# A delta-rule mixer: two of three blocks of its output gates move from ahead of the features into the solutions, states and outputs

## The chip, the core and the metric

The kernel runs on one core of a Trainium2 chip. The metric is the device time in microseconds (us) of one execution of the whole program, median of the runs. The profiles are of single executions; times in them count from the start of the profiled span.

## The reference

The program computes two two-layer transformer blocks for 256 tokens and 1024 channels in float32. The change lies in the mixer of the last layer, a gated delta rule with 8 heads of 128 channels; behind it come a mixture of experts and the final norm. Cut to what matters:

```
def gdn_mixer(h, w_in, conv_w, a_log, dt_bias, out_norm, w_out):
    proj = h @ w_in
    qkv, z, b, a = jnp.split(proj, ...)
    qkv = jax.nn.silu(causal_conv(qkv, conv_w))
    q, k, v = jnp.split(qkv, ...)
    q, k = l2_norm(q) * GDN_DK ** -0.5, l2_norm(k)
    beta = jax.nn.sigmoid(b)
    g = -jnp.exp(a_log) * jax.nn.softplus(a + dt_bias)
    o = chunk_gated_delta(q, k, v, g, beta)
    o = rms_norm(o, out_norm) * jax.nn.silu(z)
    return o @ w_out
```

Within chunk_gated_delta the cumulated decay g enters every part. The output gates silu(z) are needed only for the last product, ahead of w_out.

## The kernel before, in words

Every large product is written as three matmuls on rounded parts: an operand x is split into hi (ScalarE cast, L591) and lo = x - hi (VectorE, L592), and mm3 (L682 to L684) adds hi·hi, hi·lo and lo·hi. Weights are streamed in one fixed order (weight_order): raw tiles of up to 1024 columns are loaded by the sync queue into 8 buffers, and split in that order into 4 pairs of buffers whi and wlo, at most 4 tiles ahead of the matmuls. A split waits until the matmuls on the pair four places earlier are over.

The mixer is the function gdn. Its stages, in the order of the code:

- The normed input of the second 128 tokens is still being split (hi, lo) while the projection gdn_z begins. Its columns come in three blocks: one of 344, which are 328 gate columns and the 16 columns of b and a, and two of 348 gate columns. Each block has 8 steps (k), a step has two mm3, one for each half of the tokens (b). The results go through Silu into sz.
- From the 16 columns the decay chain is computed: the copy ab, beta by Sigmoid, then ga, ge by Abs and Exp, gl by a polynomial log1p on VectorE (L733 to L736), and g. Two matmul lines on TensorE (L2296, L2297) sum g over the tokens.
- Features (feats): six groups for k, v and q, with convolution, norm and transposes, by gdn_in weights; in between, piecewise (drip), the inverses of the triangular matrices.
- early: with the inverses done, solve for both chunks, state, correct, each for heads 0 to 3 and 4 to 7, as `four` (L2096: four 128x128 matmuls in float32, which the trace shows as 8). Then outputs(0), scales(0).
- outputs(4), scaled(0) (L2255, o times gates), scales(4), turns(0) (L2375), and then the product with gdn_out, which begins with lead.

scales ends on GpSimd with a product of the gates sz and the norm's factor (L2251), for columns 0 to 511 of sz in scales(0).

Each engine runs its own instructions in the order in which they stand. A scheduler sets that order when the program is built, from the code's order and its own estimates; it may interleave work of neighbouring parts. It put the first matmuls of the second gate block between the last ones of the first.

Of the kernel before, what the change touches and what calls it, by code (L numbers as in the profile page):

```python
# [14 lines left out]
AF = mybir.ActivationFunctionType  # L15
# [171 lines left out]
def weight_order(where, part):  # L187

    n = lambda pack: range(len(where[pack]))
    down = lambda pack: [(pack, i, where[pack][i][1] // D) for i in n(pack)]  # L190
    up = lambda pack, k=4: [(pack, i, k) for i in n(pack)]
    if part == "m0":
        first = [("ab_in", i, 8, k0) for k0 in (0, 4) for i in AB_ORDER[:FIRST]]
        return first + [("ab_in", i, 4 if i in (8, 9, 15, 16) else 8) for i in AB_ORDER[FIRST:]] + up("ab_out")
    if part == "f0":
        o = []
        for fh in range(2):
            o += [("ffn0_in", 11 * fh + j, 8) for j in range(11)]
            o += [("ffn0_out", 6 * fh + i, FF0_SPLITS[i % 3][1]) for i in range(6)]
        return o  # L200
    if part == "m1":
        return up("attn_in") + down("attn_out")
    if part == "m2":
        return up("mla_in") + up("mla_kvb", 2) + up("mla_qb") + down("mla_out")
    if part == "m3":
        return up("gdn_z") + [("gdn_in", i, 8) for i in (*range(4, 12), *range(4))] + down("gdn_out")
    if part == "f3":
        return [o for e in range(8) for o in up(f"moe_in{e}")[:10] + [(f"moe_in{e}", 10, 8)] + down(f"moe_out{e}")]
    return up(f"ffn{part[1]}_in")[:2] + up(f"ffn{part[1]}_in", 8)[2:] + down(f"ffn{part[1]}_out")
# [302 lines left out]
class Kern:  # L512
# [451 lines left out]
    def down(self, a, KC, pack, gate, job, early, pool, first=None, begun=None):  # L964

        self.tail = pool, pack, (KC - TAIL) * D
        if KC == 8:
            lead, ws, acc = begun  # L970
        else:
            acc = [[self.ps() for _ in range(2)]]
            kn = [w // D for _, w in self.where[pack]]
            ws = (w for i, n in enumerate(kn) for w in self.wk(pack, i, n))
        acc.append([self.ps() for _ in range(2)])
        mm = lambda k, w, b, hs=(0, 1): self.down_mm(a, KC, k, w, acc, b, hs)
        if KC == 8:
            for k in range(2):
                mm(k, lead[k], 1)
            if first:  # L980
                first()
        else:
            for k in range(KC - TAIL):
                w = next(ws)
                for b in range(2):
                    mm(k, w, b)
                if k == 0 and first:
                    first()
                if k in AF2:
                    self.fill()  # L990
            self.fill_all()
        last = list(enumerate(self.take(ws), KC - TAIL))
        if KC > 8:
            self.ahead(WBUFS)
        for k, w in last:
            mm(k, w, 0)
        for h in range(2):
            self.resid(self.x[:, 0], gate, h, acc[0][h])
            job.run(0, job.SQ0 + h)
        if not job.late:  # L1000
            job.run(0, job.SCALED)
        if KC == 8:
            for k in range(2, KC - TAIL):
                mm(k, lead[k], 1)
            self.ahead(WBUFS)
        for h in range(2):
            for k, w in last:
                early.get((h, k), int)()
                mm(k, w, 1, (h,))
            self.resid(self.x[:, 1], gate, h, acc[1][h])  # L1010
            job.run(1, job.SQ0 + h)
        job.run(1, job.R)
# [1057 lines left out]
    def gdn(self, mods, job):  # L2070
        nc = self.nc
        vec, act, pe, gp = nc.vector, nc.scalar, nc.tensor, nc.gpsimd
        H = 8
        with ExitStack() as es:
# [133 lines left out]
            def drip():  # L2208

                if running:  # L2210
                    r_ = running.pop(0)
                    if not next(r_, 1):
                        running.append(r_)
# [42 lines left out]

            def early():

                while running:
                    drip()  # L2260
                for f in (lambda h0: solve(0, h0), state, lambda h0: solve(1, h0), correct):
                    for h0 in (0, 4):
                        f(h0)
                outputs(0)
                scales(0)

            with ExitStack() as es2:
# [2 lines left out]
                h = job.hi, job.lo  # L2270
                h2 = job.tiles
                ab = self.t(hp, [P, 2, 2, H], "ab")
                zo = 0
                for n, z0 in enumerate((696, 0, 348)):
                    zn = (328, 348, 348)[n]
                    w = self.where["gdn_z"][2 * n][1] // 4
                    for b, acc in enumerate(self.proj(h, "gdn_z", 2 * n, w, range(2), job if n == 0 else None)):
                        act.activation(sz[:, b, z0:z0 + zn], acc[:, :zn], AF.Silu)
                        if n == 0:
                            act.copy(ab[:, b], acc[:, zn:zn + 16].rearrange("p (a h) -> p a h", a=2))  # L2280

                act.activation(beta, ab[:, :, 0], AF.Sigmoid)
                a, e, l = (self.t(hp, [P, 2, H], n) for n in ("ga", "ge", "gl"))
# [398 lines left out]
```

## Time and profile before

| what | value |
|---|---|
| median of 3 runs | 2060.82 us (2057.07 to 2062.36) |
| profiled execution, its time | 2066.18 us |
| profiled execution, its span | 2064.5 us |
| TensorE busy | 1989.5 us (96%) |
| VectorE busy | 1498.6 us (73%) |
| ScalarE busy | 1125.5 us (55%) |
| GpSimd busy | 215.3 us (10%) |
| chain that ended last | PE 79%, DVE 8%, DMA 4%, ACT 3% |

The profiled execution took 5.4 us more than the median of the runs. PE is TensorE, PEld its loading of stationary operands, DVE VectorE, ACT ScalarE, POOL GpSimd. A matmul's duration includes the way through the array, so matmuls in a row overlap: what one costs is the distance from its start to the next start. The delta-rule mixer lies between about 1405 and 1620 us.

### The profile page before, as it was taken

What the parts mean: (1) busy time and instruction counts of PE and PEld (TensorE: products, weight loads), DVE (VectorE), ACT (ScalarE), POOL (GpSimd) and SP (SyncE); (2) the same over time, 40 slices, a digit from 0 to 9 for tenths busy, and PEclk for the clock granted to TensorE, in tenths of its full rate; (3) what the DMA queues carried; (4) which work ended last, traced back from release to release, by engine and by line L of the source; (5) the groups of instructions that cost most, each with busy time, mean ns of one, the idle gap of its engine ahead of it and who ended that gap; (6) DMA issues with size and microseconds to landing.
All of it is one profiled execution on the core that took longest, in us unless ns stands there. A gap on an engine that the chain in (4) does not pass through costs nothing.

```text
span 2064.5 us, 31402 instructions
## 1 busy us (share of the span) xinstructions
PE 1989.5 (96%) x11674; PEld 1672.6 (81%) x11674; DVE 1498.6 (73%) x2378; ACT 1125.5 (55%) x1863; POOL 215.3 (10%) x359
## 2 busy tenths in 40 slices
PE   7999999999999999899998999999999899999997
PEld 4877877888888887689987779988898788878775
DVE  2667555796463358778886678877777799988996
ACT  3564462633223246764446764447645587878775
POOL 0000043000000002300001000000402201010101
PEclk8999987999999999999999999999999899999998
DMA  7313255376564233059994249995332579999995
GB/s 293 123 41 115 100 183 206 106 249 212 184 201 134 87 96 123 1 186 325 330 329 167 89 156 332 327 328 199 103 104 67 177 264 337 332 323 331 333 353 196
DMA packets 116642, 420.24 MB, mean 204 GB/s; under 512 B 13016, under 2 KB 13400, under 8 KB 116480
## 3 DMA queue, kind: packets, MB, share of 16 engines
q1 hardware_dynamic: 114640, 412.23, 57.6%
q0 software_dynamic: 976, 3.29, 0.5%
q10 hardware_dynamic: 864, 2.62, 0.3%
q8 instruction: 94, 1.54, 0.3%
q14 instruction: 68, 0.56, 0.1%
HBM read 417.04 MB, written 1.05 MB: 203 GB/s over the span
## 4 chain that ended last, share of the span: by engine, by line
PE 79%; DVE 8%; DMA 4%; ACT 3%; issue 3%; POOL 2%; SPq 0%; POOLq 0%; DVEq 0%; ACTq 0%
PE ps L682 22%; PE ps L683 21%; PE ps L684 21%; DMA raw<-in_w_ada_dram 3%; DVE wlo L592 2%; PE ps L801 2%; PE ps L1590 1%; PE ps L2096 1%; PE ps L2138 1%; DMA raw<-in_w_ffn_out_dram 1%; POOL tiny L692 1%; PE ps L2454 1%; PE ps L2568 1%; PE ps L1611 1%; PE ps L1848 1%
## 5 line engine op out<-in xcount | busy, mean ns | idle before, releaser
L592 DVE TENSOR_TENSOR wlo<-raw,whi 128x1024 fp32r<-128x1024 f32 (+1 forms) x589 | 708.3, 1223 | 171.4 <-ACT whi L591 162.7
L591 ACT CAST whi<-raw 128x1024 fp32r<-128x1024 f32 (+1 forms) x589 | 602.9, 1040 | 364.9 <-PE ps L684 178.1
L682 PE MATMUL ps<-hi,whi 128*128 128x256 f32 x832 | 239.1, 287 | 0.0
L683 PE MATMUL ps<-lo,whi 128*128 128x256 f32 x832 | 235.7, 283 | 0.0
L684 PE MATMUL ps<-hi,wlo 128*128 128x256 f32 x832 | 235.7, 283 | 0.0
L682 PE MATMUL ps<-h_hi,whi 128*128 128x512 f32 (+1 forms) x584 | 221.7, 381 | 1.9 <-ACT h_hi L591 1.9
L845 DVE SCALAR_TENSOR_TENSOR raw<-raw,acc 128x1024 f32<-128x1024 f32 x128 | 156.3, 1222 | 91.7 <-DMA raw<-in_w_ada_dram 91.2
L683 PE MATMUL ps<-h_lo,whi 128*128 128x512 f32 (+1 forms) x584 | 221.1, 379 | 0.0
L684 PE MATMUL ps<-h_hi,wlo 128*128 128x512 f32 (+1 forms) x584 | 221.0, 378 | 0.0
L682 PEld LDWEIGHTS ps<-hi,whi 128*128 128x128 f32 x832 | 159.8, 192 | 1.2
L684 PEld LDWEIGHTS ps<-hi,wlo 128*128 128x128 f32 x832 | 159.8, 192 | 0.2
L683 PEld LDWEIGHTS ps<-lo,whi 128*128 128x128 f32 x832 | 159.8, 192 | 0.1
L683 PE MATMUL ps<-wlo,hh 128*128 128x512 f32 (+1 forms) x384 | 147.0, 383 | 2.6 <-DVE wlo L592 2.5
L682 PE MATMUL ps<-whi,hh 128*128 128x512 f32 (+1 forms) x384 | 145.4, 379 | 0.0
L684 PE MATMUL ps<-whi,hl 128*128 128x512 f32 (+1 forms) x384 | 144.4, 376 | 0.0
L682 PEld LDWEIGHTS ps<-h_hi,whi 128*128 128x128 f32 x584 | 110.2, 189 | 23.4 <-ACT h_hi L591 2.0
L683 PEld LDWEIGHTS ps<-h_lo,whi 128*128 128x128 f32 x584 | 110.3, 189 | 21.9 <-DVE h_lo L592 1.7
L684 PEld LDWEIGHTS ps<-h_hi,wlo 128*128 128x128 f32 x584 | 110.2, 189 | 20.2
L683 PEld LDWEIGHTS ps<-wlo,hh 128*128 128x128 f32 x384 | 72.3, 188 | 21.0 <-DVE wlo L592 8.6
L682 PEld LDWEIGHTS ps<-whi,hh 128*128 128x128 f32 x384 | 72.4, 189 | 13.6 <-ACT hh L591 0.3
L682 PE MATMUL ps<-whi,hi 128*128 128x512 f32 (+3 forms) x208 | 80.5, 389 | 3.0 <-ACT hi L591 2.6
L684 PEld LDWEIGHTS ps<-whi,hl 128*128 128x128 f32 x384 | 72.4, 188 | 12.8
(608 smaller groups left out, 4011.1 us busy)
## 6 DMA issues: line engine op xcount, KB each, us to landing
raw<-in_w_ada_dram SPq DMA_DIRECT2D x192, 512.0 KB, 5.1
raw<-in_w_moe_in_dram SPq DMA_DIRECT2D x170, 512.0 KB, 5.7
raw<-in_w_ffn_in_dram SPq DMA_DIRECT2D x132, 512.0 KB, 5.5
raw<-in_w_moe_out_dram SPq DMA_DIRECT2D x88, 512.0 KB, 5.8
raw<-in_w_ffn_out_dram SPq DMA_DIRECT2D x64, 512.0 KB, 5.7
raw<-in_w_ab_in_dram SPq DMA_DIRECT2D x33, 512.0 KB, 4.6
raw<-in_w_gdn_in_dram SPq DMA_DIRECT2D x24, 512.0 KB, 4.5
raw<-in_w_attn_in_dram SPq DMA_DIRECT2D x12, 512.0 KB, 3.8
```

The lines of the kernel that those rows point to most:

```text
L591: self.first = self.nc.scalar.copy(hi, src)
L592: return self.nc.vector.tensor_tensor(out=lo, in0=src, in1=hi.bitcast(F32), op=ALU.subtract)
L682: mm(out, a[0], b[0], start=start, stop=False)
L683: mm(out, a[0], b[1], start=False, stop=False)
L684: return mm(out, a[1], b[0], start=False, stop=stop)
L692: self.rooted = vec.tensor_tensor(out=y, in0=v, in1=self.mhalf[:, :n], op=ALU.pow)
L801: self.moded = nc.tensor.matmul(pa[32 * g:32 * g + 32, :], self.cs[:, k, :], rw[k // 2][:, k % 2, :], start=k < 4, stop=k >= 4)
L845: nc.vector.scalar_tensor_tensor(out=t, in0=w, scalar=1.0, in1=c, op0=ALU.mult, op1=ALU.mult, accum_out=out[:, k, v:v + 1])
L1590: pe.matmul(pO[:, n], Ws[dr][:, b], mv[:, b, hd], start=True, stop=True)
L1611: pe.matmul(pS[:, b], k[:, s], q[:, s], start=True, stop=True)
L1848: pe.matmul(po[0][64 * u:64 * u + 64, n], v[:, kb, c:c + 64], PTs[u][:, kb].rearrange("p g t -> p (g t)"), start=kb == 0, stop=kb == 3)
L2096: pe.matmul(p[:, i], *f(h0 + i), start=True, stop=True)
```

## The change

The weight order and the code move blocks two and three of gdn_z behind the weights of gdn_in. The first block stays where it was. The other two become a generator, rest, whose pieces are one step (six matmuls, two mm3) each; the last piece of a block also issues its two Silu. early draws one piece after each drip and after each of the eight calls of solve, state and correct, and draws all that is left behind outputs(0) and ahead of scales(0).

```diff
@@ -203,7 +203,8 @@
     if part == "m2":
         return up("mla_in") + up("mla_kvb", 2) + up("mla_qb") + down("mla_out")
     if part == "m3":
-        return up("gdn_z") + [("gdn_in", i, 8) for i in (*range(4, 12), *range(4))] + down("gdn_out")
+        z = up("gdn_z")
+        return z[:2] + [("gdn_in", i, 8) for i in (*range(4, 12), *range(4))] + z[2:] + down("gdn_out")
     if part == "f3":
         return [o for e in range(8) for o in up(f"moe_in{e}")[:10] + [(f"moe_in{e}", 10, 8)] + down(f"moe_out{e}")]
     return up(f"ffn{part[1]}_in")[:2] + up(f"ffn{part[1]}_in", 8)[2:] + down(f"ffn{part[1]}_out")
@@ -2256,12 +2257,17 @@
 
             def early():
 
+                gates = rest()
                 while running:
                     drip()
+                    next(gates, None)
                 for f in (lambda h0: solve(0, h0), state, lambda h0: solve(1, h0), correct):
                     for h0 in (0, 4):
                         f(h0)
+                        next(gates, None)
                 outputs(0)
+                for _ in gates:
+                    pass
                 scales(0)
 
             with ExitStack() as es2:
@@ -2270,14 +2276,23 @@
                 h = job.hi, job.lo
                 h2 = job.tiles
                 ab = self.t(hp, [P, 2, 2, H], "ab")
-                zo = 0
-                for n, z0 in enumerate((696, 0, 348)):
-                    zn = (328, 348, 348)[n]
-                    w = self.where["gdn_z"][2 * n][1] // 4
-                    for b, acc in enumerate(self.proj(h, "gdn_z", 2 * n, w, range(2), job if n == 0 else None)):
-                        act.activation(sz[:, b, z0:z0 + zn], acc[:, :zn], AF.Silu)
-                        if n == 0:
-                            act.copy(ab[:, b], acc[:, zn:zn + 16].rearrange("p (a h) -> p a h", a=2))
+                for b, acc in enumerate(self.proj(h, "gdn_z", 0, 344, range(2), job)):
+                    act.activation(sz[:, b, 696:], acc[:, :328], AF.Silu)
+                    act.copy(ab[:, b], acc[:, 328:].rearrange("p (a h) -> p a h", a=2))
+
+                def rest():
+
+                    for n in (1, 2):
+                        accs = [self.ps()[:, :348] for _ in range(2)]
+                        for k, w in enumerate(w for i in range(2) for w in self.wk("gdn_z", 2 * n + i, 4)):
+                            for b in range(2):
+                                self.mm3(accs[b], [z[b][:, k] for z in h], w, k == 0, k == 7)
+                            if k < 7:
+                                yield
+                        for b in range(2):
+                            act.activation(sz[:, b, 348 * n - 348:348 * n], accs[b], AF.Silu)
+                        yield
+
 
                 act.activation(beta, ab[:, :, 0], AF.Sigmoid)
                 a, e, l = (self.t(hp, [P, 2, H], n) for n in ("ga", "ge", "gl"))
```

The names of lines below are those of the kernel before on the side of before and those of the changed kernel on its side: L682 to L684 become L683 to L685, L2096 becomes L2097, L2296 becomes L2311, L591 and L592 become L592 and L593.

TensorE at the end of the first gate block. Before, the last step of the third block (348 columns), then the sums over g, then the first features (256 columns):

```order
L683 MATMUL ps_13184<-wlo_13188,hi_6579 128x348
L684 MATMUL ps_13184<-whi_13187,lo_6580 128x348
L2296 MATMUL ps_13283<-g_12972,grp_c_2397_12969 128x8
L2297 MATMUL ps_13283<-g_12972,grp_c_2397_12969 128x8
L2296 MATMUL ps_13283<-g_12972,grp_c_2397_12969 128x8
L2297 MATMUL ps_13283<-g_12972,grp_c_2397_12969 128x8
L682 MATMUL ps_13293<-hi_6579,whi_13205 128x256
L683 MATMUL ps_13293<-lo_6580,whi_13205 128x256
```

Of the change, the same place:

```order
L683 MATMUL ps_12992<-whi_12866,hi_6579 128x344
L684 MATMUL ps_12992<-wlo_12867,hi_6579 128x344
L685 MATMUL ps_12992<-whi_12866,lo_6580 128x344
L2311 MATMUL ps_13113<-g_12972,grp_c_2397_12969 128x8
L2312 MATMUL ps_13113<-g_12972,grp_c_2397_12969 128x8
L2311 MATMUL ps_13113<-g_12972,grp_c_2397_12969 128x8
L2312 MATMUL ps_13113<-g_12972,grp_c_2397_12969 128x8
L683 MATMUL ps_13123<-hi_6579,whi_13127 128x256
```

The 96 matmuls of 348 columns that stood ahead of the sums over g are gone from this place: the sums follow directly on the first block (344 columns), and the features still stand behind them.

ScalarE at the same place, from the copy ab of the second 128 tokens to the Exp of the decay chain. Before (casts of 696 columns are of gdn_z):

```order
L2280 COPY ab_12990<-ps_12992 128x16
L591 CAST whi_13111<-raw_13109 128x696
L591 CAST whi_13129<-raw_13127 128x696
L2282 ACT_TABLE_LOAD
L2282 ACTIVATE beta_12976<-ab_12990 128x16
L591 CAST whi_13147<-raw_13145 128x696
L2286 ACTIVATE ge_13261<-ga_13260 128x16
L2287 ACT_TABLE_LOAD
L2287 ACTIVATE ge_13261<-ge_13261 128x16
```

Of the change (casts of 1024 columns are of gdn_in):

```order
L2281 COPY ab_12990<-ps_12992 128x16
L592 CAST whi_13145<-raw_13143 128x1024
L2297 ACT_TABLE_LOAD
L2297 ACTIVATE beta_12976<-ab_12990 128x16
L2301 ACTIVATE ge_13091<-ga_13090 128x16
L2302 ACT_TABLE_LOAD
L2302 ACTIVATE ge_13091<-ge_13091 128x16
```

Of three casts between the copy and the Exp one is left, a wider one; both table loads stay.

VectorE and ScalarE behind outputs(0). Of the change, ScalarE from the last feature-sized copy of outputs(0) (kT holds o) past the Silu of the third block to the copies kqT that outputs(4) reads:

```order
L2244 COPY kT_12983<-ps_15057 128x512
L724 ACTIVATE w_2747_15146<-kT_12983 128x512
L724 ACTIVATE w_2748_15149<-kT_12983 128x512
L592 CAST whi_15091<-raw_15089 128x1024
L592 CAST whi_15109<-raw_15107 128x1024
L592 CAST whi_15127<-raw_15125 128x1024
L2293 ACTIVATE sz_12971<-ps_15069 128x348
L2293 ACTIVATE sz_12971<-ps_15070 128x348
L592 CAST whi_15276<-raw_15274 128x1024
L2379 COPY kqT_12984<-ps_15157 128x4x128
L2379 COPY kqT_12984<-ps_15163 128x4x128
```

Before, the first kqT copy stood between the two Square activations (w), with no cast and no Silu in this place. VectorE, of the change, from the second half of outputs(0) to the masks LS of outputs(4):

```order
L2246 TENSOR_TENSOR kT_12983<-kT_12983,ps_15063 128x512
L725 TENSOR_REDUCE tiny_2746_15145<-w_2747_15146 128x4
L725 TENSOR_REDUCE tiny_2746_15145<-w_2748_15149 128x4
L593 TENSOR_TENSOR wlo_15092<-raw_15089,whi_15091 128x1024
L593 TENSOR_TENSOR wlo_15110<-raw_15107,whi_15109 128x1024
L593 TENSOR_TENSOR wlo_15128<-raw_15125,whi_15127 128x1024
L2256 TENSOR_TENSOR sz_12971<-kT_12983,sz_12971 128x512 x2
L593 TENSOR_TENSOR wlo_15277<-raw_15274,whi_15276 128x1024
L2132 TENSOR_TENSOR LS_12985<-ps_15170,LS_12985 128x4x128
L2132 TENSOR_TENSOR LS_12985<-ps_15176,LS_12985 128x4x128
```

Before, no subtraction of weights (wlo) stood here, and the first LS stood ahead of the first product sz. On TensorE the eight steps of the second block stand one by one behind the eight groups of solve, state and correct; the eight steps of the third block, 48 matmuls, stand in one piece between outputs(0) and the transposes and matmuls of outputs(4).

## Rows read from the trace of the kernel before

**Rows 1.** Three stretches: length, PE, PEld, DVE, ACT, POOL busy, PEclk, DMA share, GB/s

```profile
1416.00:1433.20 17.20, 17.20 (x111) 16.94 (x110) 12.57 (x28) 14.41 (x24) 0.00 (x0) 1.00 0.80 268
1433.20:1557.60 124.40, 120.43 (x1506) 115.34 (x1506) 89.86 (x187) 67.20 (x125) 28.91 (x36) 0.99 0.35 108
1557.60:1579.00 21.40, 20.51 (x178) 19.79 (x176) 15.14 (x27) 11.68 (x22) 4.78 (x8) 1.00 0.16 50
```

**Rows 2.** Timeline of TensorE, end of the output gates

```profile
1419.44 0.32 PE L682 MATMUL ps<-whi,hi 128*128 128x348 f32 x1
...
1432.25 0.32 PE L684 MATMUL ps<-whi,lo 128*128 128x348 f32 x1
1432.41 0.28 PE L2296 MATMUL ps<-g,grp_c 128*128 128x8 f32 x2
```

**Rows 3.** Groups of instructions by shape, 1405 to 1436

```profile
...
L682 PE MATMUL ps<-whi,hi 128*128 128x348 f32 x32 | 10.2, 322 | 0.0
...
L592 DVE TENSOR_TENSOR wlo<-raw,whi 128x696 fp32r<-128x696 f32 x8 | 7.0, 882 | 2.1 <-ACT whi L591 1.9
L591 ACT CAST whi<-raw 128x696 fp32r<-128x696 f32 x8 | 6.1, 771 | 0.0
...
L592 DVE TENSOR_TENSOR wlo<-raw,whi 128x1024 fp32r<-128x1024 f32 x4 | 4.8, 1222 | 0.9 <-ACT whi L591 0.9
L591 ACT CAST whi<-raw 128x1024 fp32r<-128x1024 f32 x4 | 4.2, 1048 | 1.0 <-PE ps L684 1.0
```

**Rows 4.** Timeline of VectorE, the decay chain up to g

```profile
1417.11 0.42 DVE L592 TENSOR_TENSOR lo<-w,hi 128x256 fp32r<-128x256 f32 x1
...
1424.25 0.17 DVE L733 TENSOR_SCALAR gl<-ge 128x16 f32<-128x16 f32 x1 [0.76 <-ACT ge L2287]
...
1427.85 0.17 DVE L2292 SCALAR_TENSOR_TENSOR g<-ga,tiny 128x16 f32<-128x16 f32 x1
```

**Rows 5.** Timeline of ScalarE, the same chain

```profile
1418.87 0.17 ACT L2280 COPY ab<-ps 128x16 f32<-128x16 f32 x1
...
1420.40 1.28 ACT L2282 ACT_TABLE_LOAD   x1
...
1424.00 0.22 ACT L2287 ACTIVATE ge<-ge 128x16 f32<-128x16 f32 x1
```

**Rows 6.** Timeline of TensorE, solutions to the first weights of gdn_out

```profile
1559.78 1.95 PE L2096 MATMUL ps<-vb,LS 128*128 128x128 f32 x16
1561.57 1.33 PE L2096 MATMUL ps<-vb,kt 128*128 128x128 f32 x10
...
1578.09 1.06 PE L2096 MATMUL ps<-vb,LS 128*128 128x128 f32 x8
1581.73 1.27 PE L2096 MATMUL ps<-vb,LS 128*128 128x128 f32 x8 [2.58 <-DVE LS L2131]
1582.65 0.46 PE L872 MATMUL ps<-idr,ghi 128*128 128x128 f32 x1
...
1586.09 1.85 PE L313 MATMUL ps<-grp_vecs,mod 128*128 128x8 f32 x16
```

**Rows 7.** Timelines of VectorE, ScalarE and GpSimd, the same stretch

```profile
1579.56 1.51 DVE L2255 TENSOR_TENSOR sz<-kT,sz 128x512 f32<-128x512 f32 x1 [2.48 <-POOL sz L2251]
1580.99 0.68 DVE L2131 TENSOR_TENSOR LS<-ps,LS 128x512 f32<-128x512 f32 x1
...
1574.56 0.59 ACT L2364 COPY kqT<-ps 128x512 f32<-128x512 f32 x1
...
1578.49 2.04 POOL L2251 TENSOR_TENSOR sz<-sz,tiny 128x512 f32<-128x512 f32 x2
```

**Rows 8.** Timeline of TensorE; then windows: length, PE busy, PEclk, DMA share, GB/s

```profile
1465.73 0.63 PE L2363 MATMUL ps<-grp_cc,kt 128*128 128x128 f32 x4 [2.19 <-DVE kt L2345]
...
1467.00:1468.00 1.00, 1.00 (x6) 0.50 0.01 4
...
1583.00:1584.00 1.00, 1.00 (x7) 0.50 0.00 0
```

## Prediction

> **What bounds the kernel now.** I read the windows of the mixer first, then the timelines of TensorE, ScalarE and VectorE at the two places that the change touches, then the clock of the stretches behind waits. The reader is to see that TensorE sets the pace on both sides of the move. While the gates' last two blocks are projected it is busy for all of 17.2 us, through the features and inverses nearly always, and through the solutions, states and outputs for 20.51 of 21.40 us [rows 1]. So the place that the work goes to has almost no room: 0.89 us there, and behind it one wait, from the end of the eight matmuls at 1578.09 (1578.99, at 0.112 each) to 1581.73, 2.74 us [rows 6]. The place that it leaves is where the decay chain runs: the sums over g stand at 1432.41, right behind the last gate matmul [rows 2], and g had been ready since 1428.02 [rows 4]. The sums never waited, because some 16 us of gate matmuls lay over the chain. That cover is what the change takes away, and the features are queued behind the sums.
>
> **The head, step by step.** The chain starts when the first block's second half is done, and this waits for VectorE's last piece of lo, ended at 1417.53 [rows 4]. Ahead of that piece stand two weight subtractions, and ahead of them a cast; they become 1024 wide in place of 696: 1.048 - 0.771 = 0.28 us for the cast, and 2 x (1.222 - 0.882) = 0.68 us for the subtractions [rows 3]. So lo, the end of the block and the copy ab come about 0.9 us later: ab ends at 1419.04 + 0.9 = 1419.9 [rows 5].
>
> From there to the Exp took 1424.00 - 1419.04 = 4.96 us, with ScalarE always at work [rows 5]. Three casts of 0.771 us go (2.31) and one of 1.048 stays [rows 3]: 3.70 us, the two table loads (1.28 each) among them. Exp starts at 1423.6. From the first step of log1p to the end of g took 1428.02 - 1424.25 = 3.77 us [rows 4], a subtraction of 0.882 us inside, which leaves: 2.9 us. With 0.25 us between Exp and log1p [rows 4, 5], g is there at 1426.75 and the sums can start at about 1427.0. TensorE ends the first block at about 1419.4 (0.9 us later than the block ended) and stands for some 7.6 us. It takes up the sums 1432.41 - 1427.0 = 5.4 us earlier than before, though 15.4 us of matmuls have gone. Bounds: 6.3 us earlier if lo comes no later, 4.5 us if the wider cast and subtractions of the next tiles also stand in the way.
>
> Behind such a wait the clock counts. After a wait of 2.19 us ended at 1465.73 the granted clock was 0.50, the 1.2 GHz level, in 1467 to 1468, and again in 1583 to 1584 behind the wait of 2.74 us [rows 6, 8]. Its price: the 16 groups from 1582.65 to 1586.09 took 3.44 us [rows 6]; at the 2.4 GHz level it would have been half, so one such stretch costs 1.7 us. I charge the features one: +1.7, from 0 to 2.6 (half of a stretch one and a half times as long). Features and inverses keep TensorE busy, VectorE and ScalarE have the same work, so I carry the shift unchanged to the solutions: **-5.4 + 1.7 = -3.7 us.**
>
> **The tail.** The added work: 80 matmuls from 1419.44 to 1432.25 [rows 2] are 0.160 us each; 3 x 32 of them [rows 3] are 15.4 us. Eight steps stand one by one between the groups of solve, state and correct, and these follow each other without a wait already (16 matmuls in 1561.57 - 1559.78 = 1.79 us, [rows 6]), so each step of 0.96 us pushes the next group out. The eight weight splits move too, 6.1 us on ScalarE and 7.0 us on VectorE [rows 3]; they lie between the same engines' copies, TensorE is later than they are, and ScalarE (11.68 of 21.40) and VectorE (15.14) have room [rows 1], so I price them at nothing; if they came in the way they would cost up to one split per block, 2 x 0.9 us. Their loads stand behind those of gdn_in in the queue, with 8 buffers, and the DMA share is 0.16 in that stretch [rows 1]: nothing.
>
> What the 48 matmuls of the third block remove: the wait of 2.74 us, which came from VectorE standing at its product sz (L2255) for GpSimd until 1579.56 and holding it for 1.51 us, and only then serving LS at 1580.99 [rows 7]. And the slow 3.44 us behind it, 1.7 us: **-4.4 us.**
>
> What is late next: the same chain, now hung on the end of the third block. ScalarE does two Silu (no longer than a copy of 512 columns, 0.59 us [rows 7]; the first can begin while the last matmuls run: 0.7 us together), a cast of 1.05 us whose buffer these matmuls hold, and then the kqT copy (0.59): 2.3 us after the block. TensorE has two groups of transposes for that time (0.9 us, eight matmuls as at 1578.09 [rows 6]) and waits 1.4 us. VectorE waits for GpSimd's two gate products, which wait for the Silu: 2.04 us [rows 7] from 0.3 on, its own pair 1.51 + 0.68, then a subtraction of 1.22 [rows 3], and then the two LS of 0.68: the first is done at 5.4 us. TensorE has come through three more groups by 5.0 and waits 0.4 again. Together with the restart +1.9 us; nothing if the Silu come quickly and the groups cover them, 4 us if ScalarE has fallen behind.
>
> **Sum.** 15.4 - 4.4 + 1.9 = +12.9 us in the tail, -3.7 in the head: +9.2 us. On the profiled execution's own time that is 2066.2 + 9.2 = 2075.4 us; that execution lies 5.4 us above the median of the runs, and the difference carries over to it: 2060.8 + 9.2 = **2070.0 us.**
>
> **A rule beside it.** A wait of 2.19 us was followed by the 1.2 GHz level [rows 8], so by the rows the tail's new wait of 1.4 us could bring one too: that sum is 9.2 + 1.7 = 10.9 us. The Trainium skill (TensorE: Matmul & The Clock Gate, section HAM oscillation) says that it is idle gaps above some microseconds that throw TensorE back to half rate, which it pays for at each of them. By that rule the 7.6 us in the head pay and the 1.4 us in the tail do not: 9.2 us, the sum as it stands; the trace's 2.19 us show that gaps on the short side of that rule pay too.
>
> **Rivals.** First, **hidden after all**: the sums over g don't wait, because g comes with the end of the first block. Then the head gives 1432.4 - 1419.4 = 13.0 us without a slow stretch, and 12.9 - 13.0 = -0.1 us: 2060.7, no change. With the slow stretch kept, it takes g at 1423.8 or before to bring the whole within 6.2 us. For it speaks that the chain's instructions are tiny; against it, that two table loads, a cast of 1024 and fifteen small steps on VectorE stand in order on their engines, 6.9 us from ab to g. Chance 0.05.
>
> Second, **a warm clock**: no slow stretch in the head (-1.7) and the new waits of the tail covered (-1.9): 9.2 - 3.6 = +5.6, 2066.4 us, just within what can't be told from no change. For it: the wait in the head may fall so that the level returns at once. Against it: both waits above 2 us in this mixer were followed by the low level. Chance 0.13.
>
> Third, **the splits get in the way**: the weight splits of the third block stand behind copies that wait for TensorE, and the matmuls wait for them; ScalarE falls behind, 4 us in place of 1.9, 1.8 us of splits and a second slow stretch of 1.7: 9.2 + 5.6 = +14.8, 2075.6 us. For it: VectorE stands at 71% there and in strict order. Against it: buffers come free one step after another. Chance 0.17.
>
> Fourth, **the room is larger than it looks**: VectorE, ScalarE and loads gain from 15.4 us of work taken out of the start, and the features run faster than before by what they waited, a few us of 124.4 - 120.4 = 4 us [rows 1]. Then the sum falls to +5 at best; faster than before it can hardly get, since 15.4 us of matmuls need 15.4 us of waits and the whole mixer behind the gates has 4.0 + 0.9 + 2.7 = 7.6. Chance 0.05.
>
> **From this to the numbers.** 0.3% of 2060.8 is 6.2 us, about what a measurement of this kernel can tell from no change. My forecast (0.60) and the third rival (0.17) are slower; of the forecast's own range, 2067 to 2073, all lies beyond 6.2 us. The first, second and fourth lie within it (0.23), of which I give 0.04 to faster, for a sum of them. So slower 0.77, same 0.19, faster 0.04. The range takes in the second and the third rival's price, and leaves out the first: 2064.5 to 2076.
>
> **What would show it.** Right: TensorE idle for 6 to 9 us between the last matmul of 344 columns and L2311, released by g; features some 5 us earlier, some of their first matmuls at double spacing; the groups of L2097 spread by 0.96 us each; the 2.74 us wait gone, and one of 1 to 2 us behind the 48 matmuls, released by the kqT copy. Wrong: sums over g that follow the block within 4 us (first rival), full clock behind them (second), waits within the 96 matmuls released by a split (third), or features that take less time than before from first to last (fourth).

## The result, and the profile after

The changed kernel takes 2075.56 us (median of 6 runs, 2071.16 to 2078.24); the kernel before, run beside it, 2063.91 (6 runs, 2057.07 to 2066.37). The ratio is 1.0061, 95% interval 1.0033 to 1.0089: slower by 6.8 to 18.4 us. With five more rounds on one chip it is 1.0044 (1.0025 to 1.0064), some 9.1 us. Three runs of the study that took 6168 to 10973 us are left out of every figure.

The two profiled spans, 2064.5 and 2069.3 us, differ by 4.8 us only. The difference has to be taken from a mark that both share, the transposes of kt that begin the mixer. Timeline of TensorE, before: that mark, the last transposes of kb ahead of the moved work's new place, and the next projection.

```profile
1410.10 0.77 PE L925 MATMUL ps<-grp_cc,kt 128*128 128x128 f32 x5 [1.00 <-DVE kt L916]
...
1558.88 0.63 PE L2363 MATMUL ps<-grp_cc,kb 128*128 128x128 f32 x4 [0.65 <-DVE kb L2353]
...
1588.71 0.50 PE L682 MATMUL ps<-whi,hi 128*128 128x512 f32 x1 [0.77 <-ACT hi L591]
```

The same three marks after:

```profile
1406.11 0.76 PE L926 MATMUL ps<-grp_cc,kt 128*128 128x128 f32 x5 [0.99 <-DVE kt L917]
...
1551.04 0.63 PE L2378 MATMUL ps<-grp_cc,kb 128*128 128x128 f32 x4 [0.31 <-DVE kb L2368]
...
1593.44 0.50 PE L683 MATMUL ps<-whi,hi 128*128 128x512 f32 x1 [0.77 <-ACT hi L592]
```

From mark to mark: 148.78 + 29.83 = 178.61 us before, 144.93 + 42.40 = 187.33 after. The head gave 3.85 back, the tail cost 12.57, together **+8.72**. All that the change moves lies between these marks: from the last mark to the end of the span it is 475.79 and 475.86. The 4.0 us by which the first mark is earlier after lie in code that did not change.

**The head.** TensorE after, end of the first gate block, against [rows 2]:

```profile
1414.48 0.42 PE L685 MATMUL ps<-whi,lo 128*128 128x344 f32 x1 [0.71 <-DVE lo L593]
...
1423.21 0.60 PE L2311 MATMUL ps<-g,grp_c 128*128 128x8 f32 x2 [7.84 <-DVE g L2307]
...
1425.30 0.41 PE L684 MATMUL ps<-lo,whi 128*128 128x256 f32 x1
1425.52 0.41 PE L685 MATMUL ps<-hi,wlo 128*128 128x256 f32 x1
...
1427.86 0.28 PE L684 MATMUL ps<-lo,whi 128*128 128x256 f32 x1
1427.98 0.28 PE L685 MATMUL ps<-hi,wlo 128*128 128x256 f32 x1
```

The cover is gone: a wait of 7.84 us for g, and behind it feature matmuls 0.22 us apart that are 0.12 apart some two and a half microseconds later. Windows of TensorE after (length, PE busy, PEclk, DMA share, GB/s) over the wait and behind it:

```profile
1415.11:1423.11 8.00, 0.26 (x2) 0.66 0.69 230
1423.11:1429.11 6.00, 5.90 (x32) 0.61 0.01 3
```

The chain that is waited for, VectorE and then ScalarE after, against [rows 4, 5]:

```profile
1414.00 0.42 DVE L593 TENSOR_TENSOR lo<-w,hi 128x256 fp32r<-128x256 f32 x1
...
1420.05 0.18 DVE L734 TENSOR_SCALAR gl<-ge 128x16 f32<-128x16 f32 x1 [1.93 <-ACT ge L2302]
...
1422.98 0.17 DVE L2307 SCALAR_TENSOR_TENSOR g<-ga,tiny 128x16 f32<-128x16 f32 x1
...
1415.75 0.17 ACT L2281 COPY ab<-ps 128x16 f32<-128x16 f32 x1
...
1419.80 0.21 ACT L2302 ACTIVATE ge<-ge 128x16 f32<-128x16 f32 x1
```

**The tail.** TensorE after, against [rows 6]. Six gate matmuls stand between two groups of one solution, and the 2.58 us for LS are gone; behind the 48 matmuls stand waits of 1.10 us for kqT and 0.37 us for LS:

```profile
1551.95 1.06 PE L2097 MATMUL ps<-vb,LS 128*128 128x128 f32 x8
1552.76 0.41 PE L683 MATMUL ps<-whi,hi 128*128 128x348 f32 x1
...
1553.64 0.32 PE L685 MATMUL ps<-whi,lo 128*128 128x348 f32 x1
1553.80 0.38 PE L2097 MATMUL ps<-vb,LS 128*128 128x128 f32 x2
...
1583.87 2.05 PE L2097 MATMUL ps<-kqT,kT 128*128 128x128 f32 x16 [1.10 <-ACT kqT L2379]
...
1587.19 2.05 PE L2097 MATMUL ps<-vb,LS 128*128 128x128 f32 x16 [0.37 <-DVE LS L2132]
1589.00 0.30 PE L873 MATMUL ps<-idr,ghi 128*128 128x128 f32 x1
...
1590.82 1.85 PE L314 MATMUL ps<-grp_vecs,mod 128*128 128x8 f32 x16
```

From the first matmul of L873 to the first of L314 it is 1.82 us, where [rows 6] has 3.44 at the low level: here the clock is full (the window from 1586.11 on is shown below, with the filled wait). ScalarE, VectorE and GpSimd there, against [rows 7]:

```profile
1583.23 1.08 ACT L2379 COPY kqT<-ps 128x512 f32<-128x512 f32 x2
...
1583.28 2.12 DVE L2256 TENSOR_TENSOR sz<-kT,sz 128x512 f32<-128x512 f32 x2 [0.93 <-POOL sz L2252]
...
1586.45 1.28 DVE L2132 TENSOR_TENSOR LS<-ps,LS 128x512 f32<-128x512 f32 x2
...
1582.07 2.18 POOL L2252 TENSOR_TENSOR sz<-sz,tiny 128x512 f32<-128x512 f32 x2 [3.62 <-ACT sz L2293]
```

VectorE still stands for GpSimd and serves LS behind its products, but now beside work of TensorE.

### The profile page after: what moved, and what is told of

It is laid out like the page before. It is cut to its first block, busy times and chain, and to the rows that moved or that the text cites. A ratio compares the mean times of both kernels' runs of the same rounds, so it can differ in the third digit from the quotient of the medians.

```text
span 2069.3 us, 31399 instructions
## 1 busy us (share of the span) xinstructions
PE 1985.7 (96%) x11674; PEld 1667.3 (81%) x11674; DVE 1498.1 (72%) x2378; ACT 1123.4 (54%) x1861; POOL 213.9 (10%) x359
## 4 chain that ended last, share of the span: by engine, by line
PE 75%; DVE 9%; DMA 6%; ACT 3%; issue 3%; POOL 2%; SPq 0%; POOLq 0%; DVEq 0%; ACTq 0%
PE ps L683 21%; PE ps L684 20%; PE ps L685 20%; DMA raw<-in_w_ada_dram 4%; DVE wlo L593 2%; PE ps L802 1%; DMA raw<-in_w_ffn_out_dram 1%; PE ps L1591 1%; PE ps L2139 1%; DVE raw L846 1%; POOL tiny L693 1%; PE ps L2469 1%; PE ps L2097 1%; PE ps L2583 1%; PE ps L1612 1%
## 5 line engine op out<-in xcount | busy, mean ns | idle before, releaser
L593 DVE TENSOR_TENSOR wlo<-raw,whi 128x1024 fp32r<-128x1024 f32 (+2 forms) x589 | 708.4, 1224 | 179.5 <-ACT whi L592 170.6
L592 ACT CAST whi<-raw 128x1024 fp32r<-128x1024 f32 (+2 forms) x589 | 602.6, 1040 | 351.1 <-PE ps L685 185.1
L683 PE MATMUL ps<-hi,whi 128*128 128x256 f32 x832 | 239.8, 288 | 0.0
L684 PE MATMUL ps<-lo,whi 128*128 128x256 f32 x832 | 236.2, 284 | 0.0
L685 PE MATMUL ps<-hi,wlo 128*128 128x256 f32 x832 | 236.1, 284 | 0.0
L683 PE MATMUL ps<-h_hi,whi 128*128 128x512 f32 (+1 forms) x584 | 221.2, 380 | 2.0 <-ACT h_hi L592 2.0
L684 PE MATMUL ps<-h_lo,whi 128*128 128x512 f32 (+1 forms) x584 | 221.3, 379 | 0.0
L685 PE MATMUL ps<-h_hi,wlo 128*128 128x512 f32 (+1 forms) x584 | 221.1, 379 | 0.0
L683 PEld LDWEIGHTS ps<-hi,whi 128*128 128x128 f32 x832 | 160.4, 193 | 1.2
L684 PEld LDWEIGHTS ps<-lo,whi 128*128 128x128 f32 x832 | 160.4, 193 | 0.1
L685 PEld LDWEIGHTS ps<-hi,wlo 128*128 128x128 f32 x832 | 160.3, 193 | 0.2
L684 PE MATMUL ps<-wlo,hh 128*128 128x512 f32 (+1 forms) x384 | 147.2, 383 | 2.6 <-DVE wlo L593 2.4
L683 PE MATMUL ps<-whi,hh 128*128 128x512 f32 (+1 forms) x384 | 145.6, 380 | 0.0
L685 PE MATMUL ps<-whi,hl 128*128 128x512 f32 (+1 forms) x384 | 144.3, 376 | 0.0
L683 PEld LDWEIGHTS ps<-h_hi,whi 128*128 128x128 f32 x584 | 110.1, 189 | 23.2 <-ACT h_hi L592 2.0
L684 PEld LDWEIGHTS ps<-h_lo,whi 128*128 128x128 f32 x584 | 110.3, 189 | 21.3 <-DVE h_lo L593 1.0
L685 PEld LDWEIGHTS ps<-h_hi,wlo 128*128 128x128 f32 x584 | 110.3, 189 | 20.4
L684 PEld LDWEIGHTS ps<-wlo,hh 128*128 128x128 f32 x384 | 72.4, 189 | 21.1 <-DVE wlo L593 8.8
L683 PE MATMUL ps<-whi,hi 128*128 128x512 f32 (+3 forms) x208 | 81.0, 390 | 4.1 <-ACT hi L592 3.7
L683 PEld LDWEIGHTS ps<-whi,hh 128*128 128x128 f32 x384 | 72.4, 189 | 13.7 <-ACT hh L592 0.3
L685 PEld LDWEIGHTS ps<-whi,hl 128*128 128x128 f32 x384 | 72.4, 189 | 12.7
```

The costliest lines, as they stand in the source:

```text
L592: self.first = self.nc.scalar.copy(hi, src)
L593: return self.nc.vector.tensor_tensor(out=lo, in0=src, in1=hi.bitcast(F32), op=ALU.subtract)
L683: mm(out, a[0], b[0], start=start, stop=False)
L684: mm(out, a[0], b[1], start=False, stop=False)
L685: return mm(out, a[1], b[0], start=False, stop=stop)
```

## The experiments

All marks are TensorE's, in us from the kt transposes above. "Sums" is the first sum over g, "kb" the last transposes of kb that come ahead of the solutions, "next" the first 512-column matmul of the next projection. The ratio is to the kernel before on the same chip.

| kernel | sums | kb | kb to next | next | ratio, 95% interval |
|---|---|---|---|---|---|
| before | 22.31 | 148.78 | 29.83 | 178.61 | |
| changed | 17.10 | 144.93 | 42.40 | 187.33 | 1.0061, 1.0033 to 1.0089 |
| changed, again | 17.09 | 144.90 | 42.40 | 187.30 | 1.0044, 1.0025 to 1.0064 |
| only the third block | 18.79 | 146.14 | 34.87 | 181.01 | 1.0012, 0.9984 to 1.0040 |
| only the second block | 18.78 | 148.16 | 40.42 | 188.58 | 1.0038, 1.0014 to 1.0062 |
| filled wait | 17.11 | 142.55 | 42.40 | 184.95 | 1.0041, 1.0025 to 1.0057 |
| no steps among solutions | 17.10 | 146.22 | 42.46 | 188.68 | 1.0102, 1.0046 to 1.0158 |
| later sums | 22.73 | 138.02 | 42.38 | 180.40 | 1.0037, 1.0014 to 1.0059 |
| later sums, second at keys | 22.75 | 146.78 | 34.87 | 181.65 | 1.0027, 0.9998 to 1.0055 |
| later sums, third behind outputs(0) | 26.12 | 142.05 | 34.88 | 176.93 | 1.0021, 0.9990 to 1.0053 |
| later sums, third at keys | 26.07 | 146.79 | 32.24 | 179.03 | 1.0002, 0.9977 to 1.0028 |
| ... and copies first | 26.04 | 140.42 | 34.32 | 174.74 | 0.9999, 0.9977 to 1.0020 |

Two cautions on the marks. The heads of the changed kernel and of the one with no steps among the solutions hold the same work, and so do those of the last kernel and the one with the third block behind outputs(0); yet their kb lie 1.29 and 1.63 us apart, by the clock behind the waits. So a difference below some 2 us between marks rests on the rows shown for it and not on its size. And "next" is not the end: from there to the end of the span it takes 475.79 us before and 475.86 in the changed kernel, but 477.97 with the later sums alone, 478.90 with the copies first, 479.59 with the second block at the keys and 480.00 with the filled wait. A gain at "next" is not yet a gain of the program.

**The changed kernel again**, unaltered.

> The changed kernel once more, unaltered, beside the kernel before on one chip. Theory T1 (the sum of terms read from the two traces): from the mixer on the changed kernel is 8.8 us longer (head -3.8, tail +12.6), and nothing else differs, so five rounds give +8.8 us, within about 2. Rival T2 (some further cost outside the mixer's window, or one that a single trace does not show): the +11.7 us of the medians holds or grows.

Measured: the marks repeat within 0.03 us, and the ratio gives +9.1 us (0.0025 to 0.0064 of 2066: 5.2 to 13.2). That is T1's number, and the marks have no difference outside the mixer; the interval alone would also hold T2's 11.7. The runs of one kernel spread far more than that, from 2063.07 us at a mean granted clock of 0.981 to 2082.71 at 0.972. A straight line of time against mean clock, with one slope (1.72 us per 0.001) and one offset per kernel, through the runs of this study leaves 1.8 us of scatter, and puts the changed kernel 8.5 us above the one before at equal clock. It shows what goes together and not a cause, since the low stretches behind a kernel's own waits are part of its mean clock: the filled wait lies 8.5 us above before by the runs and 11.7 by this line.

**Only the third block moves**, all of it behind outputs(0).

```diff
-        return z[:2] + [("gdn_in", i, 8) for i in (*range(4, 12), *range(4))] + z[2:] + down("gdn_out")
+        return z[:4] + [("gdn_in", i, 8) for i in (*range(4, 12), *range(4))] + z[4:] + down("gdn_out")
...
-                    next(gates, None)
...
-                        next(gates, None)
...
+                for b, acc in enumerate(self.proj(h, "gdn_z", 2, 348, range(2))):
+                    act.activation(sz[:, b, 0:348], acc, AF.Silu)
...
-                    for n in (1, 2):
+                    for n in (2,):
```

> Only the third block of the gates moves, all of it behind outputs(0); the second is projected ahead of the features again, where before has it. Theory T1 (the head gives back only what the sums over g wait for, the tail costs what is issued there): the sums still start some 5.2 us earlier, since g is ready then and some 32 of the 48 second-block matmuls (5.1 us) stand in the 7.84 us wait, which shrinks to about 2.6; the low clock behind it costs 0 to 2.1. The tail has 48 matmuls (+7.7) less the 4.4 of the gone wait and slow stretch plus 1.9 of new waits = +5.2. Sum: 0 to +2.1 us on before, 7 to 9 less than the changed kernel. Rival T2 (each block costs the same, half of the whole): +4 to +5. Rival T3 (the head is PE work, no wait takes its place): -2.5.

Timeline of TensorE:

```profile
1429.44 0.39 PE L2311 MATMUL ps<-g,grp_c 128*128 128x8 f32 x2 [4.11 <-DVE g L2307]
...
1582.09 2.05 PE L2097 MATMUL ps<-kqT,kT 128*128 128x128 f32 x16 [1.09 <-ACT kqT L2379]
```

The tail costs 5.04 us (expected 5.2): 7.7 of matmuls and 1.8 of new waits (0.37 for fT, 1.09, 0.37), less some 4.5 of wait and slow clock that are gone (4.4 charged). The head gives 2.64 where 3.1 to 5.2 were expected, and the wait is 4.11, not 2.6. ScalarE shows why:

```profile
1419.40 0.17 ACT L2279 COPY ab<-ps 128x16 f32<-128x16 f32 x1
1419.45 1.74 ACT L592 CAST whi<-raw 128x696 fp32r<-128x696 f32 x2
...
1422.62 1.99 ACT L592 CAST whi<-raw 128x1024 fp32r<-128x1024 f32 x2
...
1426.03 0.22 ACT L2302 ACTIVATE ge<-ge 128x16 f32<-128x16 f32 x1
```

Four casts lie between ab and Exp, 3.73 us, where the changed kernel has one of 1.06: two of the second block's weights and two of the features' delay g. Sum +2.40, 6.3 less than the changed kernel: nearest to T1 (0 to +2.1), with a head whose wait is mis-sized by 1.5 us. T2's 4 to 5 and T3's -2.5 both lie inside the ratio's interval; the marks speak against T2, and the waits of 4.11 and 1.09 us against T3.

**Only the second block moves**, in steps among the solutions; the third goes back ahead of the features.

```diff
+                for b, acc in enumerate(self.proj(h, "gdn_z", 4, 348, range(2))):
+                    act.activation(sz[:, b, 348:696], acc, AF.Silu)
...
-                    for n in (1, 2):
+                    for n in (1,):
```

> Only the second block moves, in eight steps among the solutions and states; the third is projected ahead of the features, so that one block of the same size as in the run with the third block alone moves, but to where no wait is filled. Theory T1 (a step among the solutions costs its six matmuls in full, and the 2.58 us wait for LS and the slow clock behind it stay): head as in that run (146.1 us from the kt transposes to the last kb transposes), tail 29.8 + 7.7 = 37.5 us, so 183.6 to the next projection, +5.0 on before's 178.6. Rival T2 (the place does not matter): 181.0 as there, +2.4.

Measured 188.58, +9.97 by the marks, twice what T1 has. The wait that T1 keeps is there:

```profile
1582.77 2.08 PE L2097 MATMUL ps<-vb,LS 128*128 128x128 f32 x8 [2.58 <-DVE LS L2132]
```

Up to this row the tail is 31.03 us, 8.18 more than before (7.7 expected; 0.35 of it is a wait for fT that before has not). Behind it the tail is 2.41 us longer, and that is clock. Windows of TensorE, this kernel and then the one before, behind the same wait:

```profile
1585.00:1588.00 3.00, 3.00 (x16) 0.50 0.03 5
...
1594.00:1596.00 2.00, 2.00 (x6) 0.50 0.00 0
```

```profile
1584.00:1587.00 3.00, 3.00 (x20) 0.66 0.03 5
1587.00:1589.00 2.00, 1.23 (x10) 1.00 0.00 0
1589.00:1591.00 2.00, 2.00 (x7) 0.62 0.00 0
1591.00:1593.00 2.00, 2.00 (x7) 0.53 0.00 0
```

It stays at 1.2 GHz up to 1596; before came back to 2.4 GHz in between. The head too is 2.0 longer than in the run with the third block alone, from the same sums (18.78) and behind nearly the same wait (4.03 against 4.11 us): there the low level lasts some 3 us (0.61 over the 4 us from the sums on), here some 6.7 us (0.50 from the sums to 1429.1). By half the time at the low level, an estimate from these windows, that is 1.7 of the 2.0 us. T2 falls, since the place decides whether a 2.58 us wait is filled. T1 has the right wait, but takes the slow stretch behind it at before's size, and that falls.

**The wait filled** with matmuls whose result nobody reads.

```diff
+                warm = self.ps()[:, :256]
+                for i in range(76):
+                    pe.matmul(warm, h2[0][:, 0, i % 8], h2[0][:, :, i % 7], start=True, stop=True)
```

> The changed kernel with 76 further matmuls (256 columns, bf16, into a PSUM tile that nobody reads: added work, not a part of the computation) between the first gate block and the sums over g. Theory T1 (the slow stretch behind the 7.84 us wait is the clock's answer to an idle TensorE): the wait is filled, g is ready at the same time, the granted clock stays at full and the first feature matmuls run at 0.12 us each at once: some 2 us less than the changed kernel. Theory T2 (the first features are slow for another reason, such as their weights): no change. If the added matmuls outlast the wait, up to 1 us is lost again.

```profile
1416.95 7.59 PE L2311 MATMUL ps<-hi 128*128 128x256 f32 x62
1424.96 0.39 PE L2315 MATMUL ps<-g,grp_c 128*128 128x8 f32 x2 [0.42 <-DVE g L2307]
...
1426.55 0.28 PE L685 MATMUL ps<-hi,wlo 128*128 128x256 f32 x1
1426.67 0.28 PE L683 MATMUL ps<-hi,whi 128*128 128x256 f32 x1
```

62 of the 76 stand in that row, the others in the shorter waits ahead of it. The sums start at the same moment (17.11), the features run 0.12 us apart at once, and kb comes 2.38 us earlier. T1: the slow features are the clock's answer to the idle TensorE. But the whole time does not come down with it, as T1 had it: 8.5 us above before (5.2 to 11.8) against the repeat's 9.1. In this trace the gain is lost again behind the tail, where the code is the same and the clock is not. The ten us from 180 behind the mark, the changed kernel and then this one:

```profile
1586.11:1596.11 10.00, 7.85 (x61) 1.00 0.18 57
```

```profile
1587.85:1597.85 10.00, 7.73 (x49) 0.82 0.09 36
```

From the first mark to the end of the span it is 664.95 us here and 663.19 in the changed kernel.

**No steps among the solutions.**

```diff
                     drip()
-                    next(gates, None)
...
                         f(h0)
-                        next(gates, None)
```

> The changed kernel with all 16 steps of the gates behind outputs(0), none among the solutions, states and corrections. Theory T1 (the solutions and states leave TensorE no wait, so a step there costs its six matmuls in full): from the mixer's first transposes of kt (line 926) to the first 512-column matmul of the next projection the time is that of the changed kernel, 187.3 us, within 0.5. Theory T2 (steps among the solutions fill some waits): longer by up to the 1.0 us that such waits add to.

kb to next, where all gate matmuls lie, is 42.46 against 42.40: the steps among the solutions fill nothing, T1. The whole, 188.68, is beyond T1's 187.3 within 0.5, but the 1.3 us more stand ahead of kb, where the work is the same: the granted clock is 0.50 in the 6 us behind the wait for g, where the changed kernel has 0.61. The ratio rests on four runs and decides nothing between the two.

**The sums later**, issued by decays() behind the first keys' projections.

```diff
             def decays():
+                yield
+                sums[0]()
                 for h0 in (0, 4):
...
+                def sum_up():
+                    pc = self.ps()[:, :32].rearrange("p (a b h) -> p a b h", a=2, b=2)
...
+                sums.append(sum_up)
```

> The changed kernel with the sums over g (8 small matmuls and the five elementwise operations behind them) issued behind the first keys' projections instead of ahead of them; nothing else changes. Theory T1 (the wait for g, not the gates, is what the moved blocks ran into): the 7.84 us wait and the 2.1 us of slow clock behind it go, so some 8 to 10 us less than the changed kernel, about 0 on before. Theory T2 (the features wait for something else that is ready no earlier, weight splits on POOL and DVE or the convolutions, which the sums only hid): the wait comes back under another name and under 4 us are gained.

Next is 6.9 us earlier than in the changed kernel, 1.8 later than before; the ratio says 1.4 less than the repeat, with wide intervals. Between T1 and T2: features run at once, but a wait comes back. TensorE, and VectorE ahead of g:

```profile
1434.56 0.39 PE L2314 MATMUL ps<-g,grp_c 128*128 128x8 f32 x2 [3.75 <-DVE g L2309]
...
1435.48 3.61 PE L2106 MATMUL ps<-grp_c,g 128*128 128x128 f32 x16
```

```profile
1427.63 0.16 DVE L737 SCALAR_TENSOR_TENSOR gl<-gl,ge 128x16 f32<-128x16 f32 x1
1427.71 0.47 DVE L2345 SCALAR_TENSOR_TENSOR cv<-ps,grp_vecs,cv 128x255 f32<-128x255 f32 x1
1428.11 0.16 DVE L737 SCALAR_TENSOR_TENSOR gl<-gl,ge 128x16 f32<-128x16 f32 x1
```

The convolutions now stand between the eleven steps of log1p, and behind the new wait the 16 matmuls of L2106 take 3.61 us, where the changed kernel's take 1.95.

**Three other places** for the blocks, each with the later sums. Second at the keys, third behind outputs(0):

```diff
+                        if not hg:
+                            for _ in rest(1):
+                                pass
...
-                for _ in gates:
+                for _ in rest(2):
```

> The sums over g behind the first keys' projections (as in the run with the later sums), the second block of the gates at the first keys' transposes, where TensorE waits 2.20 us for kt and runs at half clock after it, and the third block behind outputs(0). Measured from the first kt transposes to the next projection: before 178.6 us, later sums alone 180.4. Theory T1 (a block costs its 7.7 us less the wait that it fills): the tail loses one block (34.9 instead of 42.4 us, as in the run with the third block alone), the keys gain 7.7 less 2.2 of wait and about 1 of slow clock: 180.4 - 7.5 + 4.5 = 177.4, so about 1 us less than before. Rival T2 (the keys' wait has to be kept for the softplus steps or the convolutions, which now come later): 180 or more.

181.65: T1 missed by 4, and the number is T2's. 48 matmuls cost 8.76 us there (kb against the later sums alone). It had counted on the keys' wait of 2.20 us, and the later sums alone had already removed that one (the row is gone there too).

Second ahead of the features, third behind outputs(0):

```diff
-                    for n in (1, 2):
+                    for n in (2,):
...
+                yield
+                sums[0]()
```

> The second block ahead of the features as before, the third behind outputs(0), the sums over g behind the first keys' projections. Measured as above: before 178.6 us, third block alone 181.0. Theory T1 (the 4.1 us wait for g and the slow clock behind it are what the third block's removal left at the head): both go, 5 us less, so about 176 and 2.6 us less than before. Rival T2 (as with the later sums alone, the softplus steps stretch among the convolutions and the wait comes back at the sums): 178 to 180.

176.93, 1.68 less than before. The sums (26.12) follow without a wait and the clock stays at 1.00 around them: T1 at the head. The 1.68 us are within what the clock moves between marks, and the ratio cannot tell them from no change.

Second ahead of the features, third at the keys:

```diff
+                        if not hg:
+                            for _ in rest():
+                                pass
```

> As the run before, but the third block stands at the first keys' transposes and not behind outputs(0), so that the tail is that of before (29.8 us from the transposes of kb to the next projection). Theory T1 (fill a wait that exists: 2.2 us for kt and about 1 us of slow clock after it): head 7.7 less, keys 7.7 - 3.2 = 4.5 more, so about 175.4 and some 3 us less than before. Rival T2 (the wait for kt only moves on, to the transposes behind it): about 178.6, the same as before.

The third block costs 146.79 - 142.05 = 4.74 us there (4.5 expected): T1's number, but not its way. The kernel of the run before has no wait for kt to fill, since the later sums had removed it there as well. What it has near the keys and this one has not is a wait of 0.84 us for ScalarE and a low stretch, a mean clock of 0.83 over ten us (shown below) where this kernel has 1.00; the rest of the 4.74 was not followed up. And the tail keeps its 2.59 us wait and here pays 32.24 for before's 29.83: the windows behind it show 0.50 up to 1596, as with the second block alone. So 179.03 and not 175.4.

**The copies of q ahead of the third block**, added to the kernel with the third block behind outputs(0).

```diff
                         act.copy(dst, pt)
+                    for _ in gates:
+                        pass
+                    if typ == 0 and hg:
+                        scales(0)
```

> The kernel with the third block behind outputs(0) and the later sums, and with the transposes and copies of q for outputs(4) issued ahead of the third block instead of behind it. Theory T1 (the 1.10 us wait for the copies into kqT is new only because the gates stand between it and the work that hid it): the wait goes, 34.9 us of tail become 33.8, 175.8 us in all, 2.8 less than before. Rival T2 (the wait passes to scales(0)'s work on POOL and DVE, that is now one step later): 0.5 or less is gained.

```profile
1577.44 2.36 PE L2097 MATMUL ps<-vb,LS 128*128 128x128 f32 x16 [0.87 <-DVE LS L2132]
...
1587.63 1.22 PE L685 MATMUL ps<-whi,lo 128*128 128x512 f32 x2 [1.86 <-DVE lo L593]
```

The kqT wait is gone; the tail gains 0.56, since the wait for LS grows from 0.38 to 0.87: nearer to T2. The head's 1.6 is the clock, behind nearly the same wait for kqT (1.67 and 1.66 us). The ten us from 56 behind the mark, without this edit and with it:

```profile
1466.71:1476.71 10.00, 8.33 (x111) 0.83 0.21 60
```

```profile
1465.26:1475.26 10.00, 8.34 (x132) 1.00 0.19 57
```

Next stands 3.9 us ahead of before, but behind it VectorE makes the projection wait 1.86 us for lo (1.59 in the changed kernel), and from next to the end it takes 3.1 us more than before. The ratio is 0.9999: no kernel here is measured faster than the one before.

## Why the prediction was wrong in the time and right in the mixer

**The base failed.** The step that put the forecast at 2070.0 is "the difference carries over to it: 2060.8 + 9.2". It took the median of three runs, 2057.07 to 2062.36, for the kernel's time and the profiled execution, 2066.18, for a high one. Six runs gave a median of 2063.91, and 85 runs over this study 2065.4, so the profiled execution was an ordinary one. On the base measured beside the changed kernel the forecast is 2073.1, which takes 3.1 of the 5.6 us that it missed by. The other 2.4 are the difference of the medians, 11.65 against 9.2; the marks (+8.72) and five more rounds (+9.1) are near the forecast, but why the first six runs gave more is not shown. That the sum on the profiled execution, 2075.4, meets the measured 2075.56 is luck: its base is 2.3 us above the one measured and its difference 2.4 below.

**The head, -3.7 forecast, -3.85 found.** lo comes 0.88 us later (0.9 forecast; 7.89 against 7.01 from the mark). From ab's end to Exp it is 3.88 us (3.70), from log1p to the end of g 3.10 (2.9). The wait is 7.84 (7.6), the sums 5.21 us earlier (5.4). The slow stretch costs 2.38 us by the filled wait, where 1.7 was charged; -5.21 + 2.38 is -2.83, and 1.02 more came back further on, a term that the prediction put at nothing when it carried the shift "unchanged to the solutions". 0.34 of it is the wait for kb (0.65 before, 0.31 after), and that is no gain: a wait of 0.35 us for fT stands right behind the mark instead, in the tail. Most of the rest lies between the wait for kt and the next wait for kqT, 10.13 us before and 9.64 after. So the sum of the head is right in part by luck; the run without steps, with the same head, has -2.56.

**The tail, +12.9 forecast, +12.57 found.** A step costs its 0.96 us in full (the run without steps), the third block takes some 4.5 us away in the run with it alone (4.4), and the new waits are 1.10 and 0.37 (1.4 and 0.4). ScalarE's and VectorE's splits cost nothing to be seen: the only other wait ahead of the kqT copy is the 0.35 us for fT, that came over from kb. Here the mechanism and the terms held.

**The rivals.** The third rival's 2075.6 us is the time measured, but no wait within the 96 matmuls is released by a split, and kb to next is below the forecast, not 5.6 above: a right number by another way. The first is out by the 7.84 us. Of the second, the filled wait shows the price as 2.38 us, which the changed kernel did pay. The fourth holds at most for those 1.02 us.

**The clock.** The tail's wait of 1.10 us brought no low level: the window 1586.11 to 1596.11 after has 1.00. The 7.84 us did, with 0.61 in the 6 us behind it. The Trainium skill (TensorE: Matmul & The Clock Gate, section HAM oscillation) lets idle gaps above some microseconds throw TensorE back to half rate. These two rows agree; waits on the short side of that rule, 2.19 and 2.58 us, brought the low level too, and one of 1.67 us was followed by it in one trace while one of 1.66 us in another was not. What the prediction had from one stretch, 1.7 us for each such gap, did not hold as a size: the run with the second block alone paid 2.4 us more behind the same 2.58 us wait, up to the next projection.

## What to carry to other kernels

Work that covers a latency chain can't be taken from there at its own length: look for what runs under it and stands behind it in order. Taking 15.4 us away gave back 3.85, and moved to where TensorE had one wait it cost 12.6. Where single runs spread by tens of microseconds, measure an edit between two marks of the trace around it, and make the sum against more than three runs of the base. One repeat of the changed kernel met its marks to 0.03 us, but the same head in other kernels came out up to 1.6 us apart, so look at the clock behind each wait before a small difference is put down to the edit, and at what follows the second mark.

## What was not expected of the hardware

The same 2.58 us wait was followed by a clock that was low up to 1586 and again from some 1589.5 to 1593 in one trace (before), and without a break up to 1596 in two others (the second block alone, and the third at the keys), 2.4 us apart by the next projection. Behind waits of 4.11 and 4.03 us the low level lasted some 3 and 6.7 us, and of two waits of 1.67 and 1.66 us only one was followed by it. And the times of all kernels here go with the mean granted clock, 0.970 to 0.986 over whole runs, by 1.72 us per 0.001; from run to run that is more than any edit here did. What sets the clock of a run, or the length of a low stretch, was not tried.
